# One step of a GLA and gMLP encoder layer on one core: end of the output projection by tiles, sample states by heads

## The chip, the cores and the metric

The kernel runs on 1 core of one Trainium2 chip. The metric is device time in microseconds; the median of 3 runs of the kernel before is 2253.49 us (2249.83 to 2254.98). A core has a matrix engine (PE, with its weight loads listed as PEld), a vector engine (DVE), a scalar engine (ACT), GpSimd (POOL) and a queue engine (SP) that issues most DMAs. Each runs its own instructions in order and waits on semaphores for the others.

## The reference, cut to what matters

One mixer layer over 2048 new frames of one stream ("prompt") and 16 frames of each of 8 running streams ("sample"), width 1024:

```
h = rmsnorm(x) * (1 + scale) + shift        # shift, scale, gate from the conditioning vector
q, k, v, r, a, u, gv, z, g_a, g_b = split(h @ w_in)
o, S_new = gla_chunked(q, k, v, log_a, S0)  # 4 heads, dk 128, dv 256
y_a = (rmsnorm(o) * silu(r)) @ w_proj_a
y_b = (u * mix(layernorm(gv)) * silu(z)) @ w_proj_b
merged = sigmoid(g_a) * y_a + sigmoid(g_b) * y_b
x = x + gate * (merged @ w_out)             # the output projection
y = rmsnorm(x, final_norm_w)                # per row of 1024
```

For the sample streams S0 is a given state of 128 x 256 for each stream and head, 32 states in all; each is read, multiplied with the stream's 16 queries, added to the product of the stream's 16 keys and values, scaled and written back. All is in float32; the matrix products are done as three products of split halves (high x high, high x low, low x high).

## The kernel before, in words

The frames are 17 tiles of 128 rows: 16 of the prompt and one that holds all 8 sample streams, 16 rows each. They are worked in three groups: 6 prompt tiles, the sample tile with 4 prompt tiles, 6 prompt tiles. Each group goes through the same blocks of weights: kind S for the input projection (seven products of Strassen's kind, 12 PE matmuls each), kind P for the two branch projections, kind N for the output projection (two blocks, one for each half of 512 columns; eight jobs in a block, and each job visits all tiles of the group with three matmuls each).

`run_all` writes the program in the order of these jobs. The weight buffers `w` (nine of them) are filled by SP ahead of use. All else (attention, mixing, norms) is written as Python generators in the queue `side`; every half job calls `step()`, and one piece of a generator, up to its next `yield`, is then put into the program between the matmuls. `until` and `drain` run pieces at once, without matmuls between them. So the number of yields sets how many matmuls stand between two pieces, and where a queue is not empty at a `drain`, its rest stands in one heap.

The places that the change touches:

- `gla_gen`, the attention of one head. For the sample tile (the branch `else` of `kind == "p"`) it takes the eight states two at a time, for `p` in 0, 1, 3, 2: two products with the queries into 32 rows of `od` (L1263, float32, two passes of PE each), then six products of keys and values (L167, 32 rows of keys, so 32 rows of PE), then on DVE add (L1269), scale (L1270), and the store. `s8_load` loads six states when the head's generator begins and two more after the first two are done. The generator of the next head's decay (`la_gen`) is advanced by `next(nxt)` at a few places.
- `gate_gen`, four generators in group 0 that make the residual gate: three loads of weights on ACT's queue, for each of them three yields, up to three products into separate 32 columns of PE (L817), later a load `sel` (L824, L825), five yields, and two products `ga` (L830). They are pushed after the blocks of `gv`; the queue is drained by `pa_before(0)`, ahead of the first P job.
- The N blocks. After the last job `fin` is called for each tile: DVE multiplies by the gate (L1511), DVE or POOL adds the residual (L1512), ACT squares with a row sum (L1518). In the last group `y_gen` then runs once all is done: row sums (L1530), root on POOL (L1531, L1532), and 12 products with the norm weights (L1539) each followed by a store of 128 x 512 (L1541).

Of the kernel before, what the change touches and what calls it, by code (L numbers as in the profile page):

```python
# [16 lines left out]
D = 1024  # L17
# [90 lines left out]
def _fast_body(tc, nc, ctx, io):  # L108
# [10 lines left out]
    cst = pl("cst", 1)  # L119
    upool, spool, cpool = pl("u", 18), pl("s", 6), pl("c", 6)  # L120
    tpool, wpool = pl("wt", 3), pl("w", NW)
    sm1, sm2, sm4 = pl("sm1", 1), pl("sm2", 2), pl("sm4", 4)
    stp = pl("st", 8)
    psp = pl("ps", 8, bass.MemoryType.PSUM)
    dpool = pl("dr", 1, bass.MemoryType.DRAM)
# [256 lines left out]
    class NJob(Job):  # L382


        def src(self):
            return self.blk.raw[self.i // 2][:, 512 * (self.i % 2):512 * (self.i % 2) + 512]

        def mm(self):
            i, bk, (hi, lo) = self.i, self.blk.banks, self.blk.ops.t[self.i // 2]
            for j in range(self.blk.ops.h // 64):  # L390
                if i == 0:
                    bk[j] = PS("g")
                cols = slice(128 * j, 128 * j + 128)
                a, b = hi[:, i % 2, cols], lo[:, i % 2, cols]
                pe.matmul(bk[j], a, self.w[:, 0], start=i == 0, stop=False)  # L395
                pe.matmul(bk[j], a, self.w[:, 1], start=False, stop=False)  # L396
                pe.matmul(bk[j], b, self.w[:, 0], start=False, stop=i == 7)  # L397
                if j % 2:
                    step()

        def evac(self):
            if self.i == 7:
                for j in range(self.blk.ops.h // 64):
                    self.blk.fin(j, self.blk.banks[j])

# [394 lines left out]
    def gate_gen(q):  # L800

        nat, ts = CT(256), []

        def load(n):
            k0, k1 = KS[n]
            ts.append(S(768))
            act.dma_start(ts[n][:, 0:256 * (k1 - k0)], io["wgate"][:, 256 * (8 * q + k0):256 * (8 * q + k1)])

        load(0)
        for n, (k0, k1) in enumerate(KS):  # L810
            if n < 2:
                load(n + 1)
            for _ in range(3):
                yield
            t, ps, r = ts[n], PS("ad"), 32 * (k1 - k0)
            for k in range(k1 - k0):
                pe.matmul(ps[32 * k:32 * k + 32, 0:256], scT[:, k0 + k, :], t[:, 256 * k:256 * k + 256], start=True, stop=True)  # L817
            yield
            if n == 0:
                act.copy(nat[0:r, :], ps[0:r, 0:256])  # L820
            else:
                dve.tensor_tensor(nat[0:r, :], ps[0:r, 0:256], nat[0:r, :], ALU.add)
        sel = S(512)
# [119 lines left out]
    def make_group(g):  # L943
# [120 lines left out]
            yield  # L1064

        def qk_before(hh):
            return lambda: side.until(lambda: "k" in hd[hh])

        def qk_fin(hh):
            def f(part, hf, a, b):  # L1070
# [18 lines left out]
        def gla_gen(hh):  # L1089
# [82 lines left out]
                ahead[j] = am, kn, qj, (v[:, 0], v[:, 1])  # L1172

            def out1(j):
                oa = K2("oa", DV)
                act.activation(oa, d["o", j], AF.Copy, scale=d["rstd", j])
                d["oa", j] = oa

# [10 lines left out]
                    dve.scalar_tensor_tensor(sr[:, q, cols], tr[:, q * 128:(q + 1) * 128],  # L1189
                                             PT[:, P_GN + q:P_GN + q + 1], sr[:, q, cols], ALU.mult, ALU.mult)  # L1190

            def s8_load(p):
                for b in (2 * p, 2 * p + 1):
                    if p == 3:
                        if b == 6:
                            d["s67"] = S(2 * DV)
                        d["s8", b] = d["s67"][:, DV * (b - 6):DV * (b - 5)]
                    else:
                        d["s8", b] = sm4.tile([128, DV], F32, tag="s8", name=nm("s8"))
                    sync.dma_start(d["s8", b], io["state_gla"][0, b, hh])  # L1200

            nxt = la_gen(hh + 1) if hh < H - 1 else iter(())
            next(nxt, None)
            if has_s:
                for p in (0, 1, 3):
                    s8_load(p)
            turns(0)
            yield
            cast1(0)
# [12 lines left out]
            for j, (kind, n) in enumerate(tiles):  # L1222
# [31 lines left out]
                else:  # L1254
                    qm, es = d["qm"], d["es"]
                    od = PS("od")[:, DV:2 * DV]
                    mm(od, am, v, stop=False)
                    for p in (0, 1, 3, 2):
                        yield
                        rs = slice(32 * p, 32 * p + 32)  # L1260
                        ds = PS("at")
                        for i in range(2):
                            pe.matmul(od[rs, :], qm[:, i, rs], d["s8", 2 * p + i], start=False, stop=i == 1)  # L1263
                        for i in range(2):
                            mm(ds[:, i * DV:(i + 1) * DV], [t[rs, :] for t in kn[i]], [t[rs, :] for t in v])
                        yield
                        for i in range(2):
                            Sb = d.pop(("s8", 2 * p + i))
                            dve.tensor_tensor(Sb, ds[:, i * DV:(i + 1) * DV], Sb, ALU.add)  # L1269
                            dve.tensor_scalar(Sb, Sb, es[:, 2 * p + i:2 * p + i + 1], None, ALU.mult)  # L1270
                            sync.dma_start(io["o_ss"][0, 2 * p + i, hh], Sb)
                        if p == 0:
                            s8_load(2)
                        if p == 1:
                            next(nxt, None)
                    turns(j + 1)
                    yield
                    cast1(j + 1)
# [208 lines left out]
        def out_before(n):  # L1487
            def f():
                if n == 0:
                    side.drain()  # L1490
                    cur["yss"] = sm1.tile([128, NTM, 4], F32, tag="xss", name=nm("yss"))
                    cur["y"] = {}
                cs = slice(512 * n, 512 * n + 512)
                cur["gate"] = {}
# [12 lines left out]

        def out_fin(n):
            def f(j, ps):
                t, y = S(512), cur["y"][n, j]  # L1510
                dve.tensor_tensor(t, ps, cur["gate"][tiles[j][0]], ALU.mult)  # L1511
                (pool if j % 2 else dve).tensor_tensor(y, y, t, ALU.add)  # L1512
                if n == 0 or g + 1 == NG:
                    y_square(n, j)
            return f

        def y_square(n, j):
            act.activation(K1("sq", 512, BF16), cur["y"][n, j], AF.Square, accum_out=cur["yss"][:, j, n:n + 1])  # L1518

        def y_gen():  # L1520
# [3 lines left out]
            if g + 1 < NG:  # L1524
                for j in range(nt):
                    yield
                    y_square(1, j)
                yield
            r = sm1.tile([128, NTM], F32, tag="xrs", name=nm("yrs"))
            dve.tensor_reduce(r[:, 0:nt], cur["yss"][:, 0:nt, 0:2], AX.X, ALU.add)  # L1530
            pool.tensor_scalar(r[:, 0:nt], r[:, 0:nt], 1.0 / D, EPS, ALU.mult, ALU.add)  # L1531
            pool.tensor_tensor(r[:, 0:nt], r[:, 0:nt], neghalf.broadcast_to([128, nt]), ALU.pow)  # L1532
            yield
            for n in range(2):
                cs = slice(512 * n, 512 * n + 512)
                w = ws[n]
                for j, (kind, t) in enumerate(tiles):
                    y = cur["y"].pop((n, j))
                    dve.scalar_tensor_tensor(y, y, r[:, j:j + 1], w, ALU.mult, ALU.mult)  # L1539
                    dst = io["o_ys"].rearrange("b t d -> (b t) d") if kind == "s" else io["o_yp"][0, t * 128:t * 128 + 128]  # L1540
                    sync.dma_start(dst[:, cs], y)  # L1541
                    if g + 1 < NG or j == 2:
                        yield
                done.add(("y", g, 2 * n + 2))
                if g + 1 == NG:
                    yield

        def out_after(n):
            if n:
                return lambda: side.push(y_gen())  # L1550

        def wblk(n):
# [1294 lines left out]
```

## Time and profile before

| | |
|---|---|
| median of 3 runs | 2253.49 us |
| profiled execution, its own time | 2251.05 us |
| its span, first to last instruction | 2249.2 us |
| PE busy | 2179.8 us (97%), 13165 matmuls |
| DVE, ACT, POOL busy | 1173.7 (52%), 778.0 (35%), 677.7 us (30%) |
| DMA | 570.91 MB, mean 254 GB/s |
| mean granted clock of PE | 0.990 of 2.4 GHz |

A matmul's row gives its start and its length to the end of the pipeline; matmuls overlap, so that the distance between two starts, not the length, is what one costs. `128*32 128x256` is a stationary operand of 128 rows and 32 columns, and a moving one of 128 x 256. A row with x6 merges six neighbours, from the start of the first to the end of the last. What stands in brackets at a row's end is how long the engine stood idle before it and who released it.

### The profile page before, as it was taken

The numbers are of one execution on the slowest core, as the hardware profiler recorded it, in microseconds if no ns is written. First come the engines' busy times: TensorE is split into PE (matmuls) and PEld (weight loads), VectorE is DVE, ScalarE is ACT, GpSimd is POOL, SyncE is SP. The second block draws the span as 40 slices with busy tenths as digits, with TensorE's granted clock in tenths as the row PEclk, the third lists the DMA queues.
The fourth block names the chain that finished last, engine by engine and source line by source line (L and its number), as shares of the span: only waits on it lengthen the run. The fifth ranks groups of instructions, "written<-read, shape, count | busy, mean of one in ns | idle before, by whom it ended". The sixth has DMA issues, their size and how long they took to land. (4 is left out here: it accounts for less than half of the span.)

```text
span 2249.2 us, 35387 instructions
## 1 busy us (share of the span) xinstructions
PE 2179.8 (97%) x13165; PEld 2095.4 (93%) x13165; DVE 1173.7 (52%) x2255; ACT 778.0 (35%) x1626; POOL 677.7 (30%) x660
## 2 busy tenths in 40 slices
PE   7999999999999999999999999999999999999996
PEld 5899999999899889988899999989999999999995
DVE  6687877575548453445435236663444434324534
ACT  5555554433344332332221145433343311013322
POOL 0455555436627320110101225620111100222321
PEclk9999999999999999999999999999999999999998
DMA  7877777969966469778789886688667787674322
GB/s 302 308 294 286 294 286 295 346 251 329 345 229 220 162 241 324 266 245 270 251 307 305 291 293 235 224 273 283 228 227 243 240 273 235 223 274 146 122 90 100
DMA packets 191717, 570.91 MB, mean 254 GB/s; under 512 B 21296, under 2 KB 54704, under 8 KB 191536
## 3 DMA queue, kind: packets, MB, share of 16 engines
q1 hardware_dynamic: 186304, 560.36, 71.1%
q10 hardware_dynamic: 5040, 7.68, 1.2%
q8 instruction: 106, 1.74, 0.3%
q14 instruction: 75, 0.61, 0.1%
q0 software_dynamic: 192, 0.52, 0.1%
HBM read 396.38 MB, written 172.10 MB: 253 GB/s over the span
## 5 line engine op out<-in xcount | busy, mean ns | idle before, releaser
L326 PE MATMUL pg<-u,w 128*128 128x384 f32 (+1 forms) x2688 | 903.5, 336 | 14.6 <-DVE c L1311 4.9
L327 PE MATMUL pg<-u,w 128*128 128x384 f32 (+1 forms) x2688 | 880.4, 328 | 2.9 <-DVE u L738 2.9
L328 PE MATMUL pg<-u,w 128*128 128x384 f32 (+1 forms) x2688 | 880.7, 328 | 1.6 <-DVE w L315 1.6
L326 PEld LDWEIGHTS pg<-u,w 128*128 128x128 f32 x2688 | 507.9, 189 | 29.4 <-issue 7.8
L327 PEld LDWEIGHTS pg<-u,w 128*128 128x128 f32 x2688 | 508.2, 189 | 4.5 <-DVE u L738 3.7
L328 PEld LDWEIGHTS pg<-u,w 128*128 128x128 f32 x2688 | 507.2, 189 | 2.4 <-DVE w L315 2.1
L371 PE MATMUL pg<-u,w 128*128 128x384 f32 (+1 forms) x768 | 251.2, 327 | 0.0
L373 PE MATMUL pg<-u,w 128*128 128x384 f32 (+1 forms) x768 | 250.2, 326 | 0.5 <-DVE w L266 0.5
L372 PE MATMUL pg<-u,w 128*128 128x384 f32 (+1 forms) x768 | 250.1, 326 | 0.0
L266 DVE TENSOR_TENSOR w<-wr,w 128x512 fp32r<-128x512 f32 x144 | 158.9, 1121 | 61.2 <-ACT w L263 61.1
L373 PEld LDWEIGHTS pg<-u,w 128*128 128x128 f32 x768 | 144.2, 188 | 0.7 <-DVE w L266 0.7
L371 PEld LDWEIGHTS pg<-u,w 128*128 128x128 f32 x768 | 144.2, 188 | 0.4
L372 PEld LDWEIGHTS pg<-u,w 128*128 128x128 f32 x768 | 144.2, 188 | 0.4
L197 POOL TENSOR_SCALAR st<-st 128x1 f32<-128x1 f32 x68 | 16.1, 236 | 426.0 <-ACT sq L1112 426.0
L263 ACT CAST w<-wr 128x512 fp32r<-128x512 f32 x144 | 87.5, 617 | 134.1 <-PE pg L373 65.2
L338 ACT COPY c<-pg 128x384 f32<-128x384 f32 (+1 forms) x96 | 44.1, 459 | 198.7 <-PE pg L328 196.4
L1139 ACT CAST kn<-pat 128x128 fp32r<-128x128 f32 x68 | 18.1, 266 | 256.2 <-DVE c L1136 256.1
L397 PE MATMUL pg<-w,u 128*128 128x512 f32 x272 | 105.9, 389 | 0.0
L396 PE MATMUL pg<-w,u 128*128 128x512 f32 x272 | 105.9, 389 | 0.0
L395 PE MATMUL pg<-w,u 128*128 128x512 f32 x272 | 105.8, 389 | 0.0
L339 DVE TENSOR_TENSOR c<-pg,c 128x384 f32<-128x384 f32 (+1 forms) x96 | 51.1, 532 | 101.6 <-ACT c L338 100.0
L309 ACT CAST w<-wt 128x512 fp32r<-128x512 f32 x128 | 78.7, 621 | 73.5 <-POOL wt L288 17.9
(234 smaller groups left out, 3183.2 us busy)
## 6 DMA issues: line engine op xcount, KB each, us to landing
wr<-wb SPq DMA_DIRECT2D x64, 512.0 KB, 5.3
w<-wk_0f SPq DMA_DIRECT2D x64, 512.0 KB, 4.3
w<-wk_1f SPq DMA_DIRECT2D x64, 512.0 KB, 4.5
w<-wk_2f SPq DMA_DIRECT2D x64, 512.0 KB, 4.5
w<-wk_3f SPq DMA_DIRECT2D x64, 512.0 KB, 4.3
w<-wk_4f SPq DMA_DIRECT2D x64, 512.0 KB, 4.4
w<-wk_5f SPq DMA_DIRECT2D x64, 512.0 KB, 4.2
w<-wk_6f SPq DMA_DIRECT2D x64, 512.0 KB, 4.6
```

The costliest lines, as they stand in the source:

```text
L263: act.copy(self.w[:, 0], self.src())
L266: dve.tensor_tensor(self.w[:, 1], self.src(), self.w[:, 0].bitcast(F32), ALU.subtract)
L309: act.copy(self.w[:, 0].rearrange("p (k c) -> p k c", k=4), self.src())
L326: pe.matmul(out, w[:, 0, k, :], hi[:, k, :], start=i < 4 and k == 0, stop=False, **kw)
L327: pe.matmul(out, w[:, 0, k, :], lo[:, k, :], start=False, stop=False, **kw)
L328: pe.matmul(out, w[:, 1, k, :], hi[:, k, :], start=False, stop=k == 3, **kw)
L371: pe.matmul(out, w[:, 0, e, c], hi[:, e, ts], start=first, stop=False)
L372: pe.matmul(out, w[:, 0, e, c], lo[:, e, ts], start=False, stop=False)
L373: pe.matmul(out, w[:, 1, e, c], hi[:, e, ts], start=False, stop=end)
L395: pe.matmul(bk[j], a, self.w[:, 0], start=i == 0, stop=False)
L396: pe.matmul(bk[j], a, self.w[:, 1], start=False, stop=False)
L397: pe.matmul(bk[j], b, self.w[:, 0], start=False, stop=i == 7)
```

## The change

1. In the last N block of the program (columns 512 to 1023 of the last group) jobs 0 to 3 run as before, over all six tiles. Jobs 4 to 7 give no matmuls of their own place; at job 7 the tiles are taken one after another, each with the 12 matmuls of these four jobs and then `fin`. The residual add is on DVE for all tiles there. The norm is done tile by tile too: root on POOL for one row sum, two products with the norm weights, two stores; tile `j-1`'s follow `fin` of tile `j`. The norm weights are loaded when the block begins.
2. The eight states of a head are loaded by `qk_before`, ahead of the head's block of q and k, into five buffers `s8` (four before) and one of the shared buffers `s`. All 16 products with queries stand together, the four ranges of 32 columns in turn. The products of keys and values are done for two ranges of rows at a time, in turn, each into its own PSUM bank. `next(nxt)` follows each pair of states.
3. `oa` has one buffer, not two; `gate_gen` yields four times, not three, ahead of its products.

```diff
-    sm1, sm2, sm4 = pl("sm1", 1), pl("sm2", 2), pl("sm4", 4)
+    sm1, sm2, sm4 = pl("sm1", 1), pl("sm2", 2), pl("sm4", 5)
...
+        def tile(self, j):
+            i, bk, (hi, lo) = self.i, self.blk.banks, self.blk.ops.t[self.i // 2]
+            if i == 0:
+                bk[j] = PS("g")
+            cols = slice(128 * j, 128 * j + 128)
+            a, b = hi[:, i % 2, cols], lo[:, i % 2, cols]
+            pe.matmul(bk[j], a, self.w[:, 0], start=i == 0, stop=False)
+            pe.matmul(bk[j], a, self.w[:, 1], start=False, stop=False)
+            pe.matmul(bk[j], b, self.w[:, 0], start=False, stop=i == 7)
+
         def mm(self):
...
+            blk, nt = self.blk, self.blk.ops.h // 64
+            if blk is not blocks[-1] or self.i < 4:
+                for j in range(nt):
+                    self.tile(j)
+                    if j % 2:
+                        step()
+            elif self.i == 7:
+                for j in range(nt):
+                    for job in blk.jobs[4:8]:
+                        job.tile(j)
+                    blk.fin(j, blk.banks[j])
...
@@ gate_gen
-            for _ in range(3):
+            for _ in range(4):
                 yield
@@ qk_before
-            return lambda: side.until(lambda: "k" in hd[hh])
+            def f():
+                side.until(lambda: "k" in hd[hh])
+                if has_s:
+                    more = S(3 * DV)
+                    hd[hh]["s8"] = s8 = [sm4.tile([128, DV], F32, tag="s8", name=nm("s8")) for _ in range(5)]
+                    s8 += [more[:, DV * i:DV * i + DV] for i in range(3)]
+                    for b in range(8):
+                        sync.dma_start(s8[b], io["state_gla"][0, b, hh])
+            return f
@@ gla_gen
-                oa = K2("oa", DV)
+                oa = K1("oa", DV)
...
-            if has_s:
-                for p in (0, 1, 3):
-                    s8_load(p)
...
-                    for p in (0, 1, 3, 2):
+                    s8 = d["s8"]
+                    rows = [slice(32 * p, 32 * p + 32) for p in range(4)]
+                    yield
+                    for i in range(2):
+                        for p, rs in enumerate(rows):
+                            pe.matmul(od[rs, :], qm[:, i, rs], s8[2 * p + i], start=False, stop=i == 1)
+                    yield
+                    for pair in ((0, 1), (2, 3)):
+                        ds = {p: PS("at") for p in pair}
+                        for i in range(2):
+                            for n, (a, b) in enumerate(((0, 0), (0, 1), (1, 0))):
+                                for p in pair:
+                                    pe.matmul(ds[p][:, i * DV:(i + 1) * DV], kn[i][a][rows[p], :], v[b][rows[p], :],
+                                              start=n == 0, stop=n == 2)
                         yield
...
-                        if p == 0:
-                            s8_load(2)
-                        if p == 1:
+                        for p in pair:
+                            for b in (2 * p, 2 * p + 1):
+                                dve.tensor_tensor(s8[b], ds[p][:, b % 2 * DV:(b % 2 + 1) * DV], s8[b], ALU.add)
+                                dve.tensor_scalar(s8[b], s8[b], es[:, b:b + 1], None, ALU.mult)
+                                sync.dma_start(io["o_ss"][0, b, hh], s8[b])
                             next(nxt, None)
+                            yield
@@ out_fin
-                (pool if j % 2 else dve).tensor_tensor(y, y, t, ALU.add)
-                if n == 0 or g + 1 == NG:
+                final = n and g + 1 == NG
+                (pool if j % 2 and not final else dve).tensor_tensor(y, y, t, ALU.add)
+                if n == 0 or final:
                     y_square(n, j)
+                if final:
+                    if j > 0:
+                        y_tile(j - 1)
+                    if j + 1 == nt:
+                        y_tile(j)
+
+        def y_tile(j):
+            r = ST()
+            pool.tensor_tensor(r, cur["yss"][:, j, 0:1], cur["yss"][:, j, 1:2], ALU.add)
+            rsqrt_into(r, r, 1.0 / D)
+            for n in range(2):
+                y_out(n, j, r, cur["yw"][n])
+
+        def y_out(n, j, r, w):
+            (kind, t), y = tiles[j], cur["y"].pop((n, j))
+            dve.scalar_tensor_tensor(y, y, r, w, ALU.mult, ALU.mult)
...
+            sync.dma_start(dst[:, 512 * n:512 * n + 512], y)
...
         def out_after(n):
-            if n:
+            if n and g + 1 < NG:
                 return lambda: side.push(y_gen())
```

How the program's order moves, at three places. First PE, at the first sample tile's states (head 0), in the kernel before; `s` is a state, `x` on the right the masked queries (L1263) or keys (L167), `pat` the bank of the key products. Twelve regular matmuls stand between the two stretches:

```order
L1263 MATMUL pod_9475<-s_9395,x_9453 32x256
L1263 MATMUL pod_9475<-s_9397,x_9453 32x256
L167 MATMUL pat_9485<-v_9421,x_9457 128x256 x6
L326 MATMUL pg_9384<-u_8653,w_9283 128x320
...
L1263 MATMUL pod_9475<-s_9399,x_9453 32x256
L1263 MATMUL pod_9475<-s_9401,x_9453 32x256
L167 MATMUL pat_9521<-v_9421,x_9457 128x256 x6
```

The same place in the changed kernel:

```order
L1268 MATMUL pod_9478<-s_9234,x_9456 32x256
L1268 MATMUL pod_9478<-s_9236,x_9456 32x256
L1268 MATMUL pod_9478<-s_9238,x_9456 32x256
L1268 MATMUL pod_9478<-s_9233,x_9456 32x256
L1268 MATMUL pod_9478<-s_9235,x_9456 32x256
L1268 MATMUL pod_9478<-s_9237,x_9456 32x256
L1268 MATMUL pod_9478<-s_9233,x_9456 32x256 x2
L326 MATMUL pg_9398<-u_8653,w_9297 128x320
...
L1275 MATMUL pat_9507<-v_9424,x_9460 128x256
L1275 MATMUL pat_9508<-v_9424,x_9460 128x256
L1275 MATMUL pat_9507<-v_9424,x_9460 128x256
L1275 MATMUL pat_9508<-v_9424,x_9460 128x256
```

Four stretches of 2 + 6 instructions became one of 8 and two of 12 (the second fence shows the first four of 12); in a stretch of 12 two banks take turns.

Second PE, in group 0 at the border to the first P job, in the changed kernel: the last product of `gate_gen`'s third load (`pad`), the two products `ga` (`pga`, L840, before L830), the first P job (L371):

```order
L827 MATMUL pad_6987<-s_6873,x_99 32x256 x2
L326 MATMUL pg_6923<-u_569,w_6916 128x384
...
L328 MATMUL pg_6923<-u_569,w_6916 128x384
L840 MATMUL pga_7023<-c_6796,s_7005 128x256
L840 MATMUL pga_7028<-c_6796,s_7005 128x256
L371 MATMUL pg_7044<-u_6855,w_6949 128x384
```

Twelve regular matmuls stand between `pad` and `pga`, and none between `pga` and the P job; before, 36 stood there, and 36 more between the last `pga` and the P job, counted without the other pieces among them.

Third DVE at the end of the program, in the changed kernel: the last two tiles (L1522 and L1524 are L1511 and L1512 of before, L1543 is L1539).

```order
L1522 TENSOR_TENSOR s_22908<-pg_22729,s_22704 128x512
L1524 TENSOR_TENSOR u_22708<-u_22708,s_22908 128x512
L1543 SCALAR_TENSOR_TENSOR u_22482<-u_22482,st_22913,s_22700 128x512
L1543 SCALAR_TENSOR_TENSOR u_22708<-u_22708,st_22913,s_22701 128x512
L1522 TENSOR_TENSOR s_22933<-pg_22733,s_22704 128x512
L1524 TENSOR_TENSOR u_22708<-u_22708,s_22933 128x512
L1543 SCALAR_TENSOR_TENSOR u_22482<-u_22482,st_22938,s_22700 128x512
L1543 SCALAR_TENSOR_TENSOR u_22708<-u_22708,st_22938,s_22701 128x512
L1543 SCALAR_TENSOR_TENSOR u_22482<-u_22482,st_22946,s_22700 128x512
L1543 SCALAR_TENSOR_TENSOR u_22708<-u_22708,st_22946,s_22701 128x512
L2343 ACTIVATE x_28628<-x_28628 128x128
L2342 ACTIVATE x_28628<-x_28628 128x128
L2343 ACTIVATE x_28628<-x_28628 128x128
L2342 ACTIVATE x_28628<-x_28628 128x128
L2343 ACTIVATE x_28628<-x_28628 128x128
L2342 ACTIVATE x_28628<-x_28628 128x128
L2343 ACTIVATE x_28628<-x_28628 128x128
L2342 ACTIVATE x_28628<-x_28628 128x128
L2343 ACTIVATE x_28628<-x_28628 128x128
L2342 ACTIVATE x_28628<-x_28628 128x128
L1746 TENSOR_TENSOR wl_58020<-wr_57966,wh_58019 128x512
L2715 TENSOR_TENSOR u_57710<-u_57710,u_56568 128x256
L1746 TENSOR_TENSOR wl_58092<-wr_58017,wh_58091 128x512
L2715 TENSOR_TENSOR u_57843<-u_57843,u_56741 128x256
L1746 TENSOR_TENSOR wl_58092<-wr_58040,wh_58091 128x512
L2715 TENSOR_TENSOR u_57843<-u_57843,u_56741 128x256
L1746 TENSOR_TENSOR wl_58166<-wr_58089,wh_58165 128x512
L2715 TENSOR_TENSOR u_57843<-u_57843,u_56741 128x256
L1746 TENSOR_TENSOR wl_58166<-wr_58112,wh_58165 128x512
L2715 TENSOR_TENSOR u_57843<-u_57843,u_56741 128x256
L1817 DMA wr_52740<-w_proj_a 128x4x256
L1817 DMA wr_52786<-w_proj_a 128x4x256
L1817 DMA wr_52807<-w_proj_a 128x4x256
L1817 DMA wr_52852<-w_proj_a 128x4x256
L1817 DMA wr_52873<-w_proj_a 128x4x256
L1817 DMA wr_52918<-w_proj_a 128x4x256
L1817 DMA wr_52939<-w_proj_a 128x4x256
L1817 DMA wr_52984<-w_in 128x4x256
L1817 DMA wr_53005<-w_in 128x4x256
L1817 DMA wr_53050<-w_in 128x4x256
```

Where six multiplications and three additions stood ahead of 12 products with the norm weights, each tile now has one multiplication, one addition and the two norm products of the tile before it; the last tile has its own two as well.

## Rows read from the trace of the kernel before

**Rows 1.** Page, part 1: engine, busy us (share of the span), instructions.
```profile
PE 2179.8 (97%) x13165; PEld 2095.4 (93%) x13165; DVE 1173.7 (52%) x2255; ACT 778.0 (35%) x1626; POOL 677.7 (30%) x660
```

**Rows 2.** Waits of PE, whole span: us in total, times, longest.
```profile
PE pod L1263 <- DMA s<-state_gla: 7.2, 5, 2.6
PE pad L817 <- DMA s<-wgate: 1.6, 1, 1.6
```

**Rows 3.** Timeline of PE, one pair of states: start us, us, instruction.
```profile
896.70 0.31 PE L327 MATMUL pg<-u,w 128*128 128x320 f32 x1
896.85 0.31 PE L328 MATMUL pg<-u,w 128*128 128x320 f32 x1
897.09 1.05 PE L1263 MATMUL pod<-s,x 128*32 128x256 f32 x4
898.07 0.97 PE L167 MATMUL pat<-v,x 32*128 32x256 f32 x6
898.97 0.42 PE L326 MATMUL pg<-u,w 128*128 128x320 f32 x1
899.22 0.31 PE L327 MATMUL pg<-u,w 128*128 128x320 f32 x1
```

**Rows 4.** Line L1263: duration of one pass, ns min/median/max.
```profile
L1263 PE MATMUL pod<-s,x x64: 376/379/632, 889.4 to 1110.5; 128*32 128x256 f32 x64
```

**Rows 5.** Windows by clock: stretch, us; engines' busy (x); PEclk, DMA share, GB/s.
```profile
960.40:964.00 3.60, 3.60 (x14) 3.18 (x13) 1.47 (x4) 0.00 (x0) 0.00 (x0) 0.53 0.68 242
1100.40:1103.90 3.50, 3.50 (x11) 2.10 (x10) 1.96 (x5) 0.00 (x0) 0.00 (x0) 0.51 0.23 40
```

**Rows 6.** Timeline of PE, one of the gate's twelve stretches in group 0.
```profile
518.19 0.63 PE L817 MATMUL pad<-s,x 128*32 128x256 f32 x6
```

**Rows 7.** Timeline of DVE, a state's addition in the first head.
```profile
891.39 0.42 DVE L1269 TENSOR_TENSOR s<-pat,s 128x256 f32<-128x256 f32 x1 [2.56 <-PE pat L167]
```

**Rows 8.** Timeline of PE, the last gate and the first P job.
```profile
608.65 0.67 PE L830 MATMUL pga<-c,s 96*128 96x256 f32 x2 [1.32 <-DMA s<-kc]
...
618.21 0.33 PE L371 MATMUL pg<-u,w 128*128 128x384 f32 x1
```

**Rows 9.** Timeline of ACT, same stretch.
```profile
616.74 0.62 ACT L263 CAST w<-wr 128x512 fp32r<-128x512 f32 x1 [2.86 <-DMA wk_3f<-w]
```

**Rows 10.** Line L824, the four loads of `sel`.
```profile
DMA to landing us min/median/max: 4.7/5.1/7.3
```

**Rows 11.** Timeline of the end, all engines.
```profile
2201.76 3.10 DVE L266 TENSOR_TENSOR w<-wr,w 128x512 fp32r<-128x512 f32 x5 [2.45 <-ACT w L263]
...
2224.29 0.69 DVE L1511 TENSOR_TENSOR s<-pg,s 128x512 f32<-128x512 f32 x1 [19.43 <-PE pg L397]
...
2225.74 0.63 ACT L1518 ACTIVATE sq<-u 128x512 bf16<-128x512 f32 x1 [21.93 <-DVE u L1512]
...
2226.28 0.19 ACT L1518 ACTIVATION_READ_ACCUMULATOR sq<-u 128x1 f32 x1
...
2227.04 0.39 PE L396 MATMUL pg<-w,u 128*128 128x512 f32 x1
...
2227.26 0.39 PE L397 MATMUL pg<-w,u 128*128 128x512 f32 x1
...
2233.98 1.34 POOL L1532 TENSOR_TENSOR yrs<-yrs,nhf 128x6 f32<-128x6 f32 x1
2235.36 8.04 DVE L1539 SCALAR_TENSOR_TENSOR u<-u,yrs,s 128x512 f32<-128x512 f32 x12 [1.76 <-POOL yrs L1532]
2236.14 7.75 SPq L1541 DMA_DIRECT2D o_yp<-u  x12
```

**Rows 12.** Line L198, POOL's root of one value for each row.
```profile
L198 POOL TENSOR_TENSOR st<-st,nhf x68: 537/542/1339, 138.0 to 1813.1; 128x1 f32<-128x1 f32 x68
```

**Rows 13.** Timeline of SP's queue, the state loads of the first head.
```profile
884.62 2.79 SPq L1200 DMA_DIRECT2D s<-state_gla  x6
```

**Rows 14.** Page, part 6: DMA issues, KB each, us to landing.
```profile
w<-wk_4f SPq DMA_DIRECT2D x64, 512.0 KB, 4.4
```

More of the change, by code (lines that the diff above doesn't have):

```diff
@@ L386, in src @@
             return self.blk.raw[self.i // 2][:, 512 * (self.i % 2):512 * (self.i % 2) + 512]
-        def mm(self):
[L389 to L399, printed above, removed]
+        def tile(self, j):
[7 more added lines that the diff above has]
+            pe.matmul(bk[j], b, self.w[:, 0], start=False, stop=i == 7)
+        def mm(self):
+            blk, nt = self.blk, self.blk.ops.h // 64
[9 more added lines that the diff above has]
+                    blk.fin(j, blk.banks[j])
         def evac(self):
-            if self.i == 7:
+            if self.i == 7 and self.blk is not blocks[-1]:
                 for j in range(self.blk.ops.h // 64):
@@ L1190, in out3 @@
                                              PT[:, P_GN + q:P_GN + q + 1], sr[:, q, cols], ALU.mult, ALU.mult)
[L1192 to L1200, printed above, removed]
             nxt = la_gen(hh + 1) if hh < H - 1 else iter(())
             next(nxt, None)
-            if has_s:
-                for p in (0, 1, 3):
-                    s8_load(p)
             turns(0)
@@ L1257, in gla_gen @@
                     mm(od, am, v, stop=False)
-                    for p in (0, 1, 3, 2):
-                        yield
[L1260 to L1271, printed above, removed]
-                        if p == 0:
-                            s8_load(2)
-                        if p == 1:
+                    s8 = d["s8"]
@@ L1493, in f @@
                 cs = slice(512 * n, 512 * n + 512)
+                if n and g + 1 == NG:
+                    cur["yw"] = norm_w()
                 cur["gate"] = {}
@@ L1511, in f, with norm_w @@
                 dve.tensor_tensor(t, ps, cur["gate"][tiles[j][0]], ALU.mult)
-                (pool if j % 2 else dve).tensor_tensor(y, y, t, ALU.add)
-                if n == 0 or g + 1 == NG:
+                final = n and g + 1 == NG
+                (pool if j % 2 and not final else dve).tensor_tensor(y, y, t, ALU.add)
+                if n == 0 or final:
                     y_square(n, j)
-            return f
+                if final:
[3 more added lines that the diff above has]
+                        y_tile(j)
+            return f
+        def y_tile(j):
[7 more added lines that the diff above has]
+            dve.scalar_tensor_tensor(y, y, r, w, ALU.mult, ALU.mult)
+            dst = io["o_ys"].rearrange("b t d -> (b t) d") if kind == "s" else io["o_yp"][0, t * 128:t * 128 + 128]
+            sync.dma_start(dst[:, 512 * n:512 * n + 512], y)
         def y_square(n, j):
             act.activation(K1("sq", 512, BF16), cur["y"][n, j], AF.Square, accum_out=cur["yss"][:, j, n:n + 1])
-        def y_gen():
+        def norm_w():
             ws = [S(512), S(512)]
@@ L1523, in y_gen @@
                 sync.dma_start(ws[n], io["final_norm_w"][512 * n:512 * n + 512].partition_broadcast(128))
[L1524 to L1527, printed above, removed]
+            return ws
+        def y_gen():
+            ws = norm_w()
+            for j in range(nt):
                 yield
+                y_square(1, j)
+            yield
             r = sm1.tile([128, NTM], F32, tag="xrs", name=nm("yrs"))
@@ L1534, in y_gen @@
             for n in range(2):
[L1535 to L1543, printed above, removed]
+                for j in range(nt):
+                    y_out(n, j, r[:, j:j + 1], ws[n])
+                    yield
                 done.add(("y", g, 2 * n + 2))
-                if g + 1 == NG:
-                    yield
         def out_after(n):
-            if n:
+            if n and g + 1 < NG:
                 return lambda: side.push(y_gen())
```

## The prediction, made before the result was known

> **What bounds the kernel now.** I read the page's busy shares first: PE works 97% of the span [rows 1], so time can only be won where PE works badly, where it waits, or after its last matmul. The list of PE's waits shows two that the change aims at: 7.2 us for the states and 1.6 us for the gate's weights [rows 2]. The timeline of PE at a pair of states shows work done badly: regular matmuls start 0.15 us apart, but the four query passes and six key products take from 897.09 to 898.97 [rows 3]. The table of windows shows PE's granted clock at 0.53 and 0.51, so at the 1.2 GHz level instead of 2.4, in two short stretches of the second and fourth head, each with a wait for states ahead of it [rows 5]. The timeline of the end shows PE's last matmul starting at 2227.26 and ending at 2227.65; DVE, POOL and SP go on until 2243.89 and the span ends at 2249.2, 21.5 us after PE [rows 11].
>
> **The states of the sample tile, before.** Between the regular matmuls at 896.85 and 899.22 lie 2.37 us; without the stretch it would be two distances of 0.147, so a pair costs 2.08 us. There are 16 pairs (4 heads): 33.3 us. The waits add 7.2 [rows 2]. In the two slow windows PE did in 3.6 and 3.5 us what takes about half at full clock: some 1.6 us each, 3.2. Together 43.7 us.
>
> **The same, after.** What decides is whether products in different columns or rows of PE overlap. For columns the gate's product shows it: six passes of the same form (128 x 32 stationary, 256 moving) end 0.63 us after the first starts [rows 6], where four in one range of columns take 1.05 [rows 3]. With 0.38 us for a pass alone [rows 4], six passes are two rounds with one step of 0.25 between them, three passes to a round, while the four in one range take three steps of 0.22. So 16 passes in four ranges of columns take four rounds, the time of four passes in one range: a pair's 2.08 us without its key products (898.07 to 898.97, 0.90), 1.2 us. For ranges of rows nothing in the trace shows an overlap. If two ranges overlap, a stretch of 12 costs what six cost now, the pair's 2.08 without its query passes (897.09 to 898.07, 0.98): 1.10 us; if not, six more steps of 0.12 (0.147 x 256/320), 1.81. I take the overlap, by the nearest rows, those of the columns: per head 1.2 + 2 x 1.10 = 3.4, in all 13.6 us (without it 19.3). The loads now stand 10 weight loads of SP earlier, so I let the waits and the slow windows go. Gain 43.7 - 13.6 = 30.1 us.
>
> The row of key products, all in one range of rows [rows 3], says nothing on the point. The Trainium skill, "TensorE: Matmul & The Clock Gate", Part 3, states that products in distinct ranges of rows run at once, and gives 3.07 times for four ranges of 32 rows. By that share (0.77 of the ideal) a stretch of 12 would cost some 0.2 us more than I take, and the whole 1.7 us more; no row of this trace shows it.
>
> DVE's work is the same, but the eight state operations of two ranges follow one another (at most 8 x 0.42 = 3.4 us [rows 7]) and pieces of the next head's decay fall between them. S jobs whose banks DVE must free stand behind. From the order I count a start of about 1 us ahead of need; I put 1 us in all, between 0 and 6.
>
> **The gate in group 0.** Three more yields in each of four generators are 12 pieces, so the queue no longer empties before the first P job, and its rest is drained there: the two products `ga` now stand right ahead of L371, and the load `sel` that they wait for is issued on ACT just behind the cast that ended at 617.36 before [rows 9]. It lands 5.1 us later (4.7 to 7.3) [rows 10], at 622.5, while PE arrives at 618.2 [rows 8]. PE, which has the P jobs behind it, waits 4.3 us (3.9 to 6.5). After waits of this kind the clock fell for one stretch [rows 5], so 1.6 us more. What goes are the wait of 1.6 for weights [rows 2] and that of 1.3 for `sel` [rows 8]. Net loss 3.0 us (from a gain of 2.9 if the load comes in time, to a loss of 5.5).
>
> **The end.** Matmuls start 0.227 us apart [rows 11], so a tile's 12 take 2.7 us and DVE's four instructions for it, at 0.67 each (8.04 over 12), about as long: DVE keeps pace, and nothing but the last tile is left when PE ends. The last split of weights ended at 2204.86 [rows 11], ahead of the new need of job 7 near 2211 (2227.65 less six tiles), so PE ends when it did. The norm weights' loads stand ahead of the block's other loads on SP, and what these bring is needed only with the first tile's end, near 2214. From PE's end: 0.05 to DVE; 1.45 to the square (2224.29 to 2225.74); 0.73 for it and its read-out; three POOL instructions, at most 0.54 each [rows 12], 1.6; 0.1 to DVE; 0.78 from DVE's start to the first store and 0.67 to the second; 0.4 for its issue; and, as before, 5.3 from there to the end of the span (2243.89 to 2249.2). That is 11.1 us instead of 21.5: gain 10.4 (9 to 11.5). The root's 1.34 us for six values [rows 11] is no longer on this path for six but for one.
>
> One buffer for `oa` costs nothing: its reader on PE stands a whole tile ahead of the next writer.
>
> **Sum.** 30.1 + 10.4 - 3.0 - 1 = 36.5 us. The profiled execution took 2251.05 us, 1.85 more than its span, which gives 2214.5; the median of the runs is 2.4 above it, which gives 2217. I say 2216.
>
> **Rivals.**
> - Ranges of rows don't overlap. For it: no row shows such an overlap. Against: columns do. It costs 8 x 0.71 = 5.7 us: 2222.
> - DVE's heap of state operations holds up banks at PE, in each head about 1.5 us: 2222. For it: PE already waits for DVE at evictions, in front of the same L326. Against: DVE is busy 52% [rows 1].
> - `sel` lands in time, or the heap is spread by other waits: the gate gains 2.9 instead of losing 3.0: 2210. Against: the drain stands in the program's order.
> - The change doesn't do what it says: no product overlaps. Then a query stretch costs 15 x 0.22 + 0.5 = 3.8, a head 3.8 + 3.6, in all 30 us; gain 13.7 there and 2230 in all.
> - Slower than before. Place: SP's queue. Eight state loads (0.47 each by 2.79 for six [rows 13], 3.7 us) are issued in one piece ahead of weight loads, and the first into a shared buffer waits until it is free. Weights stand up to eight products of 1.76 us (12 x 0.147) ahead, 14 us, and land in 4.4 [rows 14]; so beyond 9.6 us of blocking in a head PE starves, and only beyond 19 us in each of four heads does it eat the 36.5. Against: the buffers are free by then, since in the order these loads wait for POOL once, and else only for older DMAs.
>
> **How the numbers follow.** Forecast 0.60; rows without overlap 0.17; DVE's heap 0.10; gate free 0.07; no overlap at all 0.04; slower 0.02. The range 2207 to 2228 holds the first four, also two of the costs together (2227) and all bounds at their good end (gate -5.9, DVE -1, end -1.1: 2208). What can be told from no change is 0.2%, 4.5 us; every case but the last lies beyond it on the fast side. Faster 0.97, within 0.2% 0.01, slower 0.02.
>
> **What would show it.** In the timeline of PE, three states' stretches per head instead of four, the one of queries about 0.9 us long from first start to last end (three steps and a pass), the stretches of 12 with starts in pairs a few ns apart, first to last start 0.6 to 0.7 us (1.3 if rows don't overlap). No wait for `state_gla`, and full clock from 880 to 1115. At the border to the first P job a wait of PE of about 4 us for `kc`, and a clock of 0.5 after it. The span's end some 11 us after PE's last matmul, with ten of twelve stores issued before that. I am wrong if PE's waits in the sample tile's stretch grow, or if the last matmul comes earlier by much else than 26 us.

## The result, and the profile after

The changed kernel takes 2219.06 us (median of four runs, 2215.63 to 2220.29), the kernel before 2254.23. The ratio is 0.9846, with a 95% interval from 0.9828 to 0.9863. The forecast was 2216. Measured again beside the experiments it took 2217.11 against 2253.99, a ratio of 0.9835 (0.9821 to 0.9850).

A correction first: in the third piece of the program's order above, the thirty rows from the first `ACTIVATE` (L2343) on don't belong there. They are rows of other engines from a second body of the program that this execution did not run; none of their lines occurs in the trace. Nothing rests on them. DVE's own rows end with the last `L1543`.

The time is spread over the program by matching the regular matmuls of S, P and N jobs: each trace has 11,184, in the same order, so the difference of two starts of the same matmul tells what was won up to there. The borders are the 2000th, 2700th, 4120th, 5200th and last one, and the end of the span. In the profile of before they lie at 469, 622, 886, 1121 and 2227 us: "gate" holds the gate generators in group 0, "sample" the four heads of the sample tile, "tail" all behind PE's last regular matmul. All numbers are us won against the one profile of before; a minus is a loss:

```
                    start   gate  between  sample  rest   tail    sum
after               -3.85  -5.43   -0.01    30.55  -1.12  10.56   30.7
after, again        -0.78  -6.47    0.83    30.55  -0.58  10.46   34.0
three yields        -1.71   1.97    0.00    30.57  -0.38  10.66   41.1
three, again        -1.01   0.85    0.65    30.57  -2.03  10.67   39.7
sel early            0.02  -3.18    0.55    30.57   0.02  10.53   38.5
rows range by range -2.61  -7.73    1.53    27.81  -0.48  10.59   29.1
queries by range     0.09  -4.64    0.22    30.48  -1.55  10.51   35.1
four ranges         -1.37  -5.69    1.54    21.59   0.14  10.69   26.9
four, spaced        -0.86  -3.56    0.00    38.32   0.05  10.55   44.5
end alone           -2.36  -0.34    0.00     0.61  -1.37  10.46    7.0
loads alone         -2.19   1.32    0.14    10.71  -1.46  -0.02    8.5
```

The first two rows are the same kernel. "Start" (0.1 to -3.9) lies ahead of every place that the change touches. In "rest" (0.1 to -2.0) only the buffer `oa` and the last block differ; the last 288 matmuls, which hold that block, win 0.0 in every kernel, and the end alone, which keeps two buffers `oa`, lost 1.4 there too. So that much is chance in one profile, and the first profile of the changed kernel had 5.0 us of it against it. No kernel beats the profile of before in the start by more than 0.1, so part of this is that profile's luck. "Sample" and "tail" repeat to 0.1 us.

The page's share of PE is unchanged beside [rows 1] (columns: busy us, share of the span, instructions):

```profile
PE 2161.4 (97%) x13165; PEld 2086.5 (94%) x13165; DVE 1174.3 (53%) x2257; ACT 778.6 (35%) x1626; POOL 678.1 (31%) x673
```

The timeline of PE at the first head's states, which answers to [rows 3] (start, duration):

```profile
897.21 0.31 PE L328 MATMUL pg<-u,w 128*128 128x320 f32 x1
897.45 1.07 PE L1268 MATMUL pod<-s,x 128*32 128x256 f32 x16
898.45 0.41 PE L326 MATMUL pg<-u,w 128*128 128x320 f32 x1
898.70 0.31 PE L327 MATMUL pg<-u,w 128*128 128x320 f32 x1
...
899.28 0.31 PE L328 MATMUL pg<-u,w 128*128 128x320 f32 x1
899.52 0.97 PE L1275 MATMUL pat<-v,x 32*128 32x256 f32 x12
900.43 0.41 PE L326 MATMUL pg<-u,w 128*128 128x320 f32 x1
900.68 0.31 PE L327 MATMUL pg<-u,w 128*128 128x320 f32 x1
```

Sixteen passes of queries take what four took, and twelve key products what six took. From 897.21 to 898.70 are 1.49 us, less two steps of 0.147: the stretch costs 1.20. The second costs 1.40 - 0.29 = 1.11. The table of windows shows the sample tile's stretch at full clock (PE busy, weight loads, DVE, ACT, POOL; granted clock, DMA share, GB/s):

```profile
880.00:1115.00 235.00, 232.16 (x1715) 225.79 (x1714) 123.02 (x368) 76.55 (x204) 30.20 (x66) 1.00 0.86 293
```

At the gate (500 to 700 us) the list of PE's waits now has these two entries, where before it had the waits for `wgate` [rows 2] and `kc` [rows 8]:

```profile
PE pga L840 <- DMA s<-kc: 5.1, 1, 5.1
PE pg L328 <- POOL w L315: 1.1, 1, 1.1
```

ACT's queue issues the load just behind the cast that [rows 9] shows in the kernel before:

```profile
618.87 0.62 ACT L263 CAST w<-wr 128x512 fp32r<-128x512 f32 x1 [3.04 <-DMA wk_3f<-w]
618.95 0.33 ACTq L834 DMA_DIRECT2D s<-kc  x1
619.33 1.18 ACTq L835 DMA_DIRECT2D s<-b_ada  x1
```

PE reaches the two products at 619.8 and starts them when the load is there, 6.0 us after its issue; behind them stands the first P job, and the window after shows the granted clock at 0.51, the 1.2 GHz level:

```profile
619.48 0.34 PE L328 MATMUL pg<-u,w 128*128 128x384 f32 x1
624.91 1.97 PE L840 MATMUL pga<-c,s 96*128 96x256 f32 x4 [5.09 <-DMA s<-kc]
626.32 0.88 PE L371 MATMUL pg<-u,w 128*128 128x384 f32 x1
```
```profile
624.90:628.40 3.50, 3.49 (x10) 3.15 (x11) 1.84 (x4) 0.30 (x1) 0.00 (x0) 0.51 0.23 79
```

The end, which answers to [rows 11], all engines, the last tile only:

```profile
2198.78 14.50 SPq L1545 DMA_DIRECT2D o_yp<-u  x12
...
2207.13 0.39 PE L396 MATMUL pg<-w,u 128*128 128x512 f32 x1
...
2207.55 0.69 DVE L1522 TENSOR_TENSOR s<-pg,s 128x512 f32<-128x512 f32 x1
...
2209.06 0.63 ACT L1548 ACTIVATE sq<-u 128x512 bf16<-128x512 f32 x1 [2.00 <-DVE u L1524]
...
2209.86 0.48 POOL L1536 TENSOR_TENSOR st<-yss 128x1 f32<-128x1 f32 x1 [1.32 <-ACT sq L1548]
2210.43 0.19 POOL L197 TENSOR_SCALAR st<-st 128x1 f32<-128x1 f32 x1
2210.71 0.55 POOL L198 TENSOR_TENSOR st<-st,nhf 128x1 f32<-128x1 f32 x1
2211.30 1.42 DVE L1543 SCALAR_TENSOR_TENSOR u<-u,st,s 128x512 f32<-128x512 f32 x2 [1.00 <-POOL st L198]
```

The first of the 12 stores is issued at 2198.78, 8.7 us before PE's end; the span ends at 2218.5, 11.0 us after PE's last matmul (2207.52).

### The profile page after: what moved, and what is told of

Same layout as the page of the kernel before. It is cut to its first block, busy times and chain, and to the rows that moved or that the text cites. A ratio compares the mean times of both kernels' runs of the same rounds, so it can differ in the third digit from the quotient of the medians.

```text
span 2218.5 us, 35445 instructions
## 1 busy us (share of the span) xinstructions
PE 2161.4 (97%) x13165; PEld 2086.5 (94%) x13165; DVE 1174.3 (53%) x2257; ACT 778.6 (35%) x1626; POOL 678.1 (31%) x673
## 5 line engine op out<-in xcount | busy, mean ns | idle before, releaser
L371 PE MATMUL pg<-u,w 128*128 128x384 f32 (+1 forms) x768 | 251.9, 328 | 0.0
L371 PEld LDWEIGHTS pg<-u,w 128*128 128x128 f32 x768 | 144.5, 188 | 0.5
L309 ACT CAST w<-wt 128x512 fp32r<-128x512 f32 x128 | 78.7, 621 | 72.6 <-POOL wt L290 19.7
```

The source lines that it names most:

```text
L309: act.copy(self.w[:, 0].rearrange("p (k c) -> p k c", k=4), self.src())
L371: pe.matmul(out, w[:, 0, e, c], hi[:, e, ts], start=first, stop=False)
```

## Experiments

The theory: the gain comes from the states (products in different columns and rows of PE overlap, and the loads come in time) and from the end. Against it stands a loss at the gate, where pieces drained in one heap put a late load on PE's path. The rivals are that ranges of rows don't overlap, that DVE's heap of state operations holds up PE, and that the loss at the gate is chance.

**The changed kernel again.** 

> The changed kernel once more, as the measure for the runs beside it. In its first trace the last matmul comes 20.1 us earlier than before, the span ends 30.7 us earlier, and 3.8 us of loss lie in the first 140 us, which the change does not touch. If those 3.8 us are chance (which loads come late at the start), the difference of the medians is nearer 34.5 us: 2219. If they belong to the change, this profile shows them again and the difference is 31: 2223.

It took 2217.11 us (0.9835, 0.9821 to 0.9850), 36.9 less than the kernel before beside it: below both figures, on the side of chance. The start costs 0.8 instead of 3.85, so most of that was chance. The wait for `kc` was 6.1 this time, and the granted clock stood at 0.50 for 6.8 us:

```profile
620.20:627.00 6.80, 4.68 (x13) 4.35 (x14) 2.05 (x4) 1.35 (x2) 0.15 (x1) 0.50 0.40 133
```

**Three yields in the gate generators**, all else as changed:

```diff
-            for _ in range(4):
+            for _ in range(3):
                 yield
```

> Three yields instead of four in the gate generators, all else as changed. Theory (the heap at the drain): the wait of 5.1 us for the load at the first P job and the half clock of 1.7 us behind it go, the waits of 1.6 for the gate's weights and 1.3 for the earlier load come back: 5.5 us faster than the changed kernel, near 2213.5. Rival (the two traces differ there by chance): the same as the changed kernel, 2219.

It took 2209.95 us (0.9808, 0.9794 to 0.9821), 7.2 less than the changed kernel beside it, where 5.5 had been expected. It was measured again:

> The kernel with three yields once more, as the measure for the run beside it, and to see whether its lead over the changed kernel (2209.95 against 2217.11 beside it) holds: 2210 if it does.

This time it took 2211.38 us (0.9812, 0.9799 to 0.9826). PE's waits at the gate, in the first profile:

```profile
PE pad L827 <- DMA s<-wgate: 0.7, 1, 0.7
PE pga L840 <- DMA s<-kc: 0.3, 1, 0.3
```

The wait at the P job and the slow stretch behind it are gone, and the waits that came back are smaller than in the profile of before. So the fourth yield is a loss of its own, some 7 us. Of the five profiles with four yields and the late load, all lose 4.6 to 7.7 us at the gate. Of the six with three yields, counting before, five lie between -0.3 and 2.0, and one (four, spaced) lost 3.6. There the waits for the same loads, 1.9 and 1.8, are 0.8 longer than before, and the granted clock stood at 0.50 for 6.8 us from 472.9, where before it did for 3.4, and for 3.4 us more from 568.5.

**The late load issued earlier**, with four yields (its three lines are taken out behind the loop):

```diff
                 load(n + 1)
+            else:
+                sel = S(512)
+                act.dma_start(sel[:, 0:256], ...)
+                act.dma_start(sel[:, 256:512], ...)
             for _ in range(4):
                 yield
```

> Four yields as changed, but the load of the gate's selection table and bias is issued one load of weights earlier, ahead of the last four yields. Theory (only the late load costs): no wait at the first P job, full clock there, no wait for gate weights: 5.1 + 1.7 = 6.8 us faster than the changed kernel, 2212. Rival (the buffer that the load goes into comes free only late, or the pieces at the drain themselves cost): the wait stays, 2219.

It took 2211.75 us (0.9816, 0.9801 to 0.9831). By time the theory holds, by the trace only half of it. The wait for `kc` fell to 0.4, but another took its place:

```profile
PE pg L326 <- DVE c L342: 2.6, 1, 2.6
PE pga L841 <- DMA s<-kc: 0.4, 1, 0.4
```

The timelines of ACT, POOL and DVE show the chain. ACT's sequencer stood from 607.9 to 611.4 at a semaphore ahead of the load; its next cast and DVE's subtraction behind that cast came late, and the eviction L342 for PE stood behind this subtraction:

```profile
611.42 0.34 ACTq L825 DMA_DIRECT2D s<-kc  x1
611.79 0.47 ACTq L826 DMA_DIRECT2D s<-b_ada  x1
612.30 0.83 ACT L160 CAST u<-s 128x768 fp32r<-128x768 f32 x1 [3.75 <-POOL u L161]
```
```profile
609.55 1.84 POOL L161 TENSOR_TENSOR u<-s,u 128x768 fp32r<-128x768 f32 x1
```
```profile
613.17 0.96 DVE L161 TENSOR_TENSOR u<-s,u 128x768 fp32r<-128x768 f32 x1 [4.39 <-ACT u L160]
614.04 0.55 DVE L342 TENSOR_TENSOR c<-pg,c 128x384 f32<-128x384 f32 x1
```

Behind the wait the granted clock was 0.50 again, for 6.8 us from 616.2. The gate still lost 3.2 us. The semaphore that came last was POOL's: its L161, which reads one of the buffers `s` as the load fills one, ended at 611.39, and the load was issued 0.03 us later. So the rival, a buffer that comes free late, is read from the trace; it wasn't tried apart.

**Key products range by range**, not in turn:

```diff
-                        for i in range(2):
-                            for n, (a, b) in enumerate(...):
-                                for p in pair:
+                        for p in pair:
+                            for i in range(2):
+                                for n, (a, b) in enumerate(...):
```

> The 12 products of a stretch stand range by range (six of one range of rows, then six of the other) instead of in turn; same banks, same places. Theory (ranges overlap only between neighbours in the queue): starts 0.12 us apart within a range, six more steps, 0.7 us more for each of 8 stretches: 5.7 us slower than the changed kernel, 2225. Rival (PE overlaps them in any order, or not at all): no difference, 2219.

It took 2220.18 us (0.9841, 0.9824 to 0.9859): by time not to be told from the changed kernel. The sample's stretch tells it: 27.81 won instead of 30.55, so 2.7 us slower, half of the theory. The stretch is 0.35 us longer, where six more steps would be 0.7:

```profile
898.81 0.31 PE L328 MATMUL pg<-u,w 128*128 128x320 f32 x1
899.05 1.32 PE L1275 MATMUL pat<-v,x 32*128 32x256 f32 x12
900.30 0.41 PE L326 MATMUL pg<-u,w 128*128 128x320 f32 x1
```

So PE begins products of the second range while the first range still has some to come, but not at once. That ranges of rows overlap is shown; that only neighbours in the queue do is wrong. The order within the stretch is worth half of what the theory gave it.

**Query products range by range:**

```diff
-                    for i in range(2):
-                        for p, rs in enumerate(rows):
+                    for p, rs in enumerate(rows):
+                        for i in range(2):
```

> The 16 passes of a head's query products stand range by range of columns (four passes of one range, then the next) instead of in turn. Theory (columns overlap only between neighbours): 12 steps of 0.22 us instead of three, 2.0 to 2.6 us more in each of four heads: 8 to 10 us slower than the changed kernel, 2227 to 2229. Rival (the order within the 16 is of no weight): 2219.

It took 2218.43 us (0.9832, 0.9815 to 0.9849), and the sample's stretch won 30.48 us. The theory fell, the rival holds: the 16 passes take 1.09 us (1.07 in turn). The trace has the first passes of the four ranges 13 ns apart, in turn 7 ns, so the order in the queue did change:

```profile
892.50 1.09 PE L1268 MATMUL pod<-s,x 128*32 128x256 f32 x16
893.52 0.41 PE L326 MATMUL pg<-u,w 128*128 128x320 f32 x1
```

Four passes of one range behind one another need three steps of 0.22; were the ranges begun in the queue's order, 12 such steps would take 2.6 us. For these query passes it counts that all four ranges stand in one stretch, not their order in it.

**Four ranges of rows at once**, four banks:

```diff
-                    for pair in ((0, 1), (2, 3)):
+                    for pair in ((0, 1, 2, 3),):
```

> The products of keys and values of all four ranges of 32 rows in one stretch of 24, four PSUM banks in turn, instead of two stretches of 12. Theory (four ranges run side by side as two do): a stretch of 24 takes what one of 12 takes now, 1.0 us, so 1.0 us less in each of four heads: 4 us faster than the changed kernel, 2215. Rival 1 (only two ranges at a time): the stretch takes 1.9 us, no gain. Rival 2 (four banks held until DVE has read them all): PE waits for banks behind it, some us slower.

It took 2224.25 us (0.9871, 0.9854 to 0.9887), 7.1 more than the changed kernel beside it. On PE the theory holds: 24 products take 0.98 us. Yet the heads became longer, by waits for DVE that were not there and by longer ones for `oa` (2.8 in the changed kernel); around and behind the first the granted clock was 0.61. The stretch of PE with that window, and PE's waits from 870 to 1130 us:

```profile
895.75 0.98 PE L1275 MATMUL pat<-v,x 32*128 32x256 f32 x24
...
903.43 0.42 PE L326 MATMUL pg<-u,w 128*128 128x320 f32 x1 [2.12 <-DVE c L1320]
```
```profile
903.00:907.40 4.40, 3.96 (x17) 3.97 (x18) 2.70 (x8) 0.97 (x5) 0.00 (x0) 0.61 0.99 308
```
```profile
PE pg L326 <- DVE c L1320: 6.5, 4, 2.1
PE ptr L1201 <- ACT oa L1194: 5.5, 3, 1.8
```

DVE's timeline names the cause: six states (the last is shown) and the first pieces of the next head's decay stand ahead of L1320, which PE waits for. In the changed kernel L1320 stands behind the fourth state.

```profile
900.37 0.41 DVE L1280 TENSOR_TENSOR s<-pat,s 128x256 f32<-128x256 f32 x1
900.82 0.35 DVE L1281 TENSOR_SCALAR s<-s,st 128x256 f32<-128x256 f32 x1
901.09 0.82 DVE L1048 TENSOR_TENSOR s<-s,s 128x640 f32<-128x640 f32 x1
901.94 0.42 DVE L1052 TENSOR_TENSOR_SCAN s<-kcf,s 128x128 f32<-128x128 f32 x1
902.28 0.71 DVE L1052 TENSOR_TENSOR_SCAN s<-scanpf,s 128x128 f32<-128x128 f32 x2
902.91 0.47 DVE L1320 TENSOR_TENSOR c<-pg,c 128x320 f32<-128x320 f32 x1
```

This is the forecast's rival of DVE's heap, in a kernel where it decides. Whether it was the order on DVE or the four banks is told apart by the next.

**Four ranges, spaced**, on the kernel with three yields:

```diff
+                    for pair in ((0, 1, 2, 3),):
...
                             next(nxt, None)
                             yield
+                            if p < 3:
+                                yield
```

> Three yields in the gate generators, the key products of all four ranges of rows in one stretch of 24, and one more yield after each pair of states, so that DVE's read of an S job's bank stands after the fourth state and not after the sixth. Theory (in the stretch of 24 the PE work was as short as hoped, and only DVE's order made PE wait): no wait of 2 us for DVE's read in any head, 1.0 us less in each of four heads than with three yields alone: 2206. Rival (four banks at a time are too many, whatever DVE's order): PE waits for banks again, 2212 or more.

It took 2206.35 us (0.9785, 0.9771 to 0.9799), 5.0 less than three yields alone beside it, and is the fastest of all. PE waits for nothing from 870 to 1130 us. The eviction (here L1322) now stands behind the fourth state:

```profile
898.28 0.35 DVE L1281 TENSOR_SCALAR s<-s,st 128x256 f32<-128x256 f32 x1
898.55 0.48 DVE L1322 TENSOR_TENSOR c<-pg,c 128x320 f32<-128x320 f32 x1
898.95 0.42 DVE L1280 TENSOR_TENSOR s<-pat,s 128x256 f32<-128x256 f32 x1
```

So the order on DVE was the cause, not the banks, of which four are still taken at once. The sample's stretch won 7.8 us on top of 30.57: 4 from the stretches, 2.8 from a wait for `oa` (L1194) that the later places removed too; the last 1.0 isn't accounted for. This profile lost 3.6 us at the gate, by chance as far as the others show. So that the time came out at the 2206 expected is in part luck: the stretch won more than the 4 us of the theory, and the gate gave some back.

**The end alone**, on the kernel before: jobs 4 to 7 and the norm tile by tile, states and gate as before.

> The kernel before with the end tile by tile alone (states, gate and buffers as before). Theory: the span ends 11 us after PE's last matmul instead of 21.5, and nothing else moves: 10.4 us faster than before, 2243.8. Rival (the parts help each other): less than 9 or more than 12.

It took 2243.92 us (0.9950, 0.9934 to 0.9966), 11.4 less than before; in its profile the tail won 10.46 and the sample's stretch 0.6. The page's span and PE's last matmul:

```profile
span 2242.2 us, 35398 instructions
```
```profile
2230.72 0.39 PE L396 MATMUL pg<-w,u 128*128 128x512 f32 x1
```

**The loads alone**, on the kernel before: eight loads in `qk_before`, five buffers `s8`, one `oa`; products in pairs as before.

> The kernel before with the eight states of a head loaded a block ahead alone; products in pairs of states as before, 16 stretches. Theory: the 7.2 us of waits for states go, and with them the two windows at half clock (3.2): 10.4 us faster, 2243.8. Rival 1 (the clock falls there for another reason): 7.2 us, 2247. Rival 2 (eight loads in a row hold up the weights on SP's queue): less, or slower.

It took 2242.50 us (0.9940, 0.9924 to 0.9955), 12.8 less. No wait for states is left, the granted clock from 880 to 1115 is full, and the stretch won 10.71:

```profile
880.00:1115.00 235.00, 232.16 (x1574) 216.13 (x1573) 116.86 (x345) 70.08 (x187) 27.60 (x59) 1.00 0.83 268
```

The loads are 10.7 of the 30.55, the overlap and the fewer stretches the other 19.8 (33.3 - 13.6 = 19.7 in the forecast). No run takes these two apart; by the forecast's price without any overlap, 30 us, some 16 of the 19.8 would be overlap, an estimate. SP's queue held nothing up: the first rival's 7.2 us and the second's slower kernel both fall.

## Why the prediction was right, point by point

- **States: right.** 4 x (1.20 + 2 x 1.11) = 13.7 us of stretches, forecast 13.6 (the queries' is 1.07 us from first start to last end, not 0.9). The stretch won 30.55, forecast 30.1; the loads alone are 10.7 where 7.2 of waits and 3.2 of slow clock had been put.
- **Rows overlap: right, and more than I used.** No row of before showed it; I took it from the columns, a guess that came true. Four ranges do it as well as two: 24 products take 0.98 us, 12 take 0.97. In one range 24 would take, by an estimate from the 0.97 us of six and 18 more steps of 0.12, 3.1 us, which is 3.2 times as long. The Trainium skill, "TensorE: Matmul & The Clock Gate", Part 3, gives 3.07 times for four ranges, with 512 moving columns. The trace, with 256, comes near it. The 0.2 us more for a stretch of 12 that the forecast worked out from that figure did not show: 1.11 us, where 1.10 was put.
- **DVE's heap: 1 us forecast, none found** in the changed kernel: no wait for DVE from 870 to 1130 us. With six states ahead of the eviction instead of four, the sample's stretch lost 9 us net (four ranges). The margin was one pair of states.
- **The gate: right in place and sign, too small.** The step that was mis-sized is "net loss 3.0 us". It measured 5.4 and 6.5 in the two profiles of the changed kernel, beyond the far bound that its own terms give (6.5 + 1.6 - 2.9 = 5.2; the 5.5 stated is a slip). The wait was 5.1 and 6.1, not 4.3: PE arrived 0.9 us after the load's issue in the first profile, as forecast, but the load took 5.8 to land and not 5.1; the slow clock was one stretch of 3.4 us, or one of 6.8 with PE busy for 4.68 of it, which costs about half of that, 2.3 us, and not 1.6; and a wait of 1.1 for a weight split on POOL (L315) came that no step had. What was given back, 1.6 and 1.3, varies between profiles: three yields showed 0.7 and 0.3, or 1.9 and 1.8. Why L315 is late there was not traced.
- **The end: right.** 11.0 us after PE instead of the 11.1 forecast; 10.5 won, forecast 10.4. Alone on before it won the same, so it rests on no other part. Two small readings were off: 0.54 us is the median in [rows 12], not the most (1.34), yet the three POOL instructions took 1.4 us, less than the 1.6 put; and seven stores, not ten, are issued before PE's end, the tenth 2.8 us after it.
- **One buffer for `oa`: right.** PE's wait for `oa` from 870 to 1130 us is 2.8 us in both kernels.
- **The last matmul** was to come 26 us earlier, and by my own test "much else" would make me wrong: it came 20.1 earlier in one profile and 23.5 in the other. Of the missing 5.9 the gate is 2.4, chance outside the change 5.0 (start 3.85, rest 1.1), and the states gave back 1.5.
- **The sum.** 30.5 + 10.5 - 6 = 35 us, beside 35.2 and 36.9 between medians; forecast 36.5. States, heap and gate missed by 0.4, 1 and 2.4 to 3.5, partly against one another, so that the total came out so close is in part luck. Two slips: the sum gives 2217, not the 2216 said; and with no overlap at all it gives 2216 + 30.1 - 13.7 = 2232, not 2230, still outside the range.

The forecast's way to 2210, a gate without loss, is what the kernel with three yields shows: 2209.95.

## What to carry to other kernels

Gather products that use different columns or rows of PE into one stretch: here a stretch of two or four ranges cost what one range had cost. Let ranges of rows take turns in it; one behind the other they cost 0.35 us more. Then look at what the engine behind it must read in a heap, and leave a place in it for the eviction that PE waits for next. Where a generator's yields are added, follow the last pieces of the queue to where it is drained: here PE waited 5.1 of the 6.0 us from the issue of a load there, and the granted clock was at half for 3.4 us behind it.

## What was not expected of the hardware

- PE starts passes for other columns ahead of earlier ones in its queue that wait for their own: 16 passes took 1.09 us range by range and 1.07 in turn. The Trainium skill, "TensorE: Matmul & The Clock Gate", Part 3, says that matmuls start and end strictly in the order of the queue; here the measurement differs. For rows PE does so only in part: 1.32 us range by range, 0.97 in turn.
- The same kind of wait at the same place left the clock at its lower level for 3.4 us in one execution and for 6.8 in another, there partly within the wait (waits of 5.1 and 6.1 us). In the kernel with the early load a wait of 2.6 was followed by 6.8 us as well. Why the lengths differ was not traced.
